# A row-wise log-softmax gradient: loads and stores grouped by two, one row sum moved from VectorE to ScalarE, synchronization by hand

## The chip, the cores and the metric

The kernel runs on one core of one Trainium2 chip. The metric is device time in microseconds (us), lower is better. A profile is one further look at one execution. Its engine names are DVE (VectorE), ACT (ScalarE), POOL (GpSimd) and SP (SyncE, which here only issues transfers; SPq is its queue). The DMA engines are 16 units that share each transfer.

## The reference

`y` and `dy` are float32 of shape 8 x 1024 x 8192, that is 8192 rows of 8192 elements; the output has the same shape.

```python
def reference(y, dy):
    softmax_x = np.exp(y)
    sum_dy = np.sum(dy, axis=-1, keepdims=True)
    return (dy - softmax_x * sum_dy).astype(np.float32)
```

Two inputs are read once and one output is written once: 3 x 268.44 MB = 805.3 MB. No version can move less.

## The kernel before

Rows are taken in G = 32 groups of 256, two rows (R = 2) to a partition. A `dy` tile is 64 KB per partition and has two buffers; the two `y` tiles are 32 KB each. That makes 192 KB of each partition, so a `dy` buffer must be stored before it can be loaded again. All transfers are issued by SyncE on one queue. VectorE takes the negated sums of both rows in one reduction; ScalarE takes the exponential in place; VectorE adds the product to `dy` in place. A framework inserts the waits.

```python
    def load_dy(g):
        dy_t = dyp.tile([P, R * D], fp32, name="dy_t")
        nc.sync.dma_start(out=dy_t[:], in_=dy_v[g])
        s_t = stats.tile([P, R], fp32, name="s_t")
        nc.vector.tensor_reduce(
            out=s_t[:],
            in_=dy_t[:].rearrange("p (r d) -> p r d", r=R),
            axis=mybir.AxisListType.X,
            op=ALU.add,
            negate=True,
        )
        return dy_t, s_t

    def load_y(g):
        y_ts = []
        for r in range(R):
            y_t = yp.tile([P, D], fp32, name="y_t")
            nc.sync.dma_start(out=y_t[:], in_=y_v[g][:, r * D : (r + 1) * D])
            y_ts.append(y_t)
        return y_ts

    def compute(dy_t, s_t, y_ts):
        for r in range(R):
            for c in range(0, D, CD):
                e = y_ts[r][:, c : c + CD]
                d = dy_t[:, r * D + c : r * D + c + CD]
                nc.scalar.activation(e, e, EXP)
                nc.vector.scalar_tensor_tensor(
                    out=d, in0=e, scalar=s_t[:, r : r + 1], in1=d, op0=ALU.mult, op1=ALU.add
                )

    def store(g, dy_t, parts=1):
        w = R * D // parts
        for k in range(parts):
            nc.sync.dma_start(
                out=out_v[g][:, k * w : (k + 1) * w], in_=dy_t[:, k * w : (k + 1) * w]
            )

    cur = load_dy(0)
    for g in range(G):
        if g < G - 1:
            y_ts = load_y(g)
            compute(*cur, y_ts)
            nxt = load_dy(g + 1)
            if g < G - 2:
                store(g, cur[0])
                cur = nxt
            else:
                held, cur = cur, nxt
        else:
            y_ts = load_y(g)
            compute(*cur, y_ts)
            store(g - 1, held[0])
            store(g, cur[0], parts=R)
# (cut: the launch)
```

In the steady state the queue reads: store of group g, the two `y` halves of g+1, `dy` of g+2, then the next store.

## Time and profile before

| | before |
|---|---|
| time, median | 1866.9 us (1866.81 to 1867.58, 3 runs) |
| span of the profiled run | 1865.4 us |
| DMA queue, share of the 16 engines' time | 99.9% |
| mean rate | 432 GB/s |
| VectorE / ScalarE busy | 60% / 25% |

The page of the kernel before: busy time of each engine (us, share of the span, number of instructions), the DMA rows of the 40-slice picture (tenths of busy time, then GB/s), the total, and the queue table (packets, MB, share of the 16 engines).

```profile
DVE 1119.2 (60%) x160; ACT 457.1 (25%) x129; POOL 0.2 (0%) x4
...
DMA  9999999999999999999999999999999999999999
GB/s 427 416 434 431 443 433 422 435 437 436 427 433 431 440 430 434 431 429 441 433 437 425 433 442 431 434 425 436 438 434 433 428 434 437 437 431 430 429 435 396
DMA packets 18582, 805.36 MB, mean 432 GB/s; under 512 B 2064, under 2 KB 2064, under 8 KB 2064
...
q1 hardware_dynamic: 18576, 805.31, 99.9%
...
DMA 74%; DVE 17%; ACT 6%; SPq 1%; issue 1%; DVEq 0%; ACTq 0%
```

The DMA row never leaves 9 and the queue holds the engines 99.9% of the span. VectorE and ScalarE have room. The last line is the chain of waits, followed back from the last instruction, by engine: it gives VectorE 17% of the span.

The timeline of the kernel before over one group (start, duration, engine, line, operation, out<-in, shapes, count; in brackets the idle time just before and what ended it):

```profile
113.31 0.34 SPq L77 DMA_DIRECT2D out_dram<-dy_t  x1
113.75 0.86 SPq L60 DMA_DIRECT2D y_t<-in_y_dram  x2
120.33 17.22 DVE L47 TENSOR_REDUCE s_t<-dy_t 128x2 f32<-128x16384 f32 x1 [7.04 <-DMA dy_t<-in_dy_dram]
139.66 0.33 SPq L45 DMA_DIRECT2D dy_t<-in_dy_dram  x1
```

The store is issued at 113.31 us, while the `dy` load ahead of it is still landing: that landing releases the reduction at 120.33 us. So the store stood in the queue 7.0 us before the previous transfer had landed. The next `dy` load is issued at 139.66 us, when the store has completed; the two `y` loads issued at 113.75 us keep the engines busy until it gets its turn.

### The profile page before, as it was taken

The page shows a single profiled execution, that of the slowest core. Times are in us where ns is not written, and L with a number is a line of the kernel's source. Part 1 is how long each engine was busy: PE and PEld are TensorE (multiplying, and loading weights), DVE is VectorE, ACT ScalarE, POOL GpSimd, SP SyncE. Part 2 cuts the span into 40 slices and gives each one's busy share as a digit, 9 for nine tenths or more (in the row PEclk, how much of TensorE's full clock was granted, in tenths as well). Part 3 has the DMA queues.
Part 4 walks back from the last instruction along what each step waited for, and adds up shares of the span by engine and source line. Part 5 has one row for each costly group of instructions (what it writes and reads, how often), then busy time and mean ns, then how long its engine had stood idle before and what let it go on. Part 6 is the DMA issues. An engine that isn't in the chain of part 4 may idle for free.

```text
span 1865.4 us, 712 instructions
## 1 busy us (share of the span) xinstructions
DVE 1119.2 (60%) x160; ACT 457.1 (25%) x129; POOL 0.2 (0%) x4
## 2 busy tenths in 40 slices
DVE  5675555755557555575555755657656576565664
ACT  2123321233212332123321233212332113331132
POOL 0000000000000000000000000000000000000000
DMA  9999999999999999999999999999999999999999
GB/s 427 416 434 431 443 433 422 435 437 436 427 433 431 440 430 434 431 429 441 433 437 425 433 442 431 434 425 436 438 434 433 428 434 437 437 431 430 429 435 396
DMA packets 18582, 805.36 MB, mean 432 GB/s; under 512 B 2064, under 2 KB 2064, under 8 KB 2064
## 3 DMA queue, kind: packets, MB, share of 16 engines
q1 hardware_dynamic: 18576, 805.31, 99.9%
q14 instruction: 6, 0.05, 0.0%
HBM read 536.87 MB, written 268.44 MB: 432 GB/s over the span
## 4 chain that ended last, share of the span: by engine, by line
DMA 74%; DVE 17%; ACT 6%; SPq 1%; issue 1%; DVEq 0%; ACTq 0%
DMA y_t<-in_y_dram 69%; DVE dy_t L70 15%; ACT y_t L69 6%; DMA dy_t<-in_dy_dram 3%; DVE s_t L47 2%; DMA out_dram<-dy_t 1%; SPq L60 1%; SPq L77 1%; DVEq L122 0%; ACTq L69 0%; DVEq L70 0%
## 5 line engine op out<-in xcount | busy, mean ns | idle before, releaser
L70 DVE SCALAR_TENSOR_TENSOR dy_t<-y_t,s_t,dy_t 128x4096 f32<-128x4096 f32 x128 | 568.1, 4481 | 490.3 <-ACT y_t L69 490.1
L69 ACT ACTIVATE y_t<-y_t 128x4096 f32<-128x4096 f32 x128 | 455.9, 3608 | 1375.6 <-DMA y_t<-in_y_dram 1375.6
L47 DVE TENSOR_REDUCE s_t<-dy_t 128x2 f32<-128x16384 f32 x32 | 551.0, 17220 | 232.1 <-DMA dy_t<-in_dy_dram 232.1
L69 ACT ACT_TABLE_LOAD x1 | 1.3, 1283 | 0.7 <-PEq L111 0.7
L111 POOL MEMSET const-bfloat16-1.0<- 128x1 bf16 x1 | 0.1, 102 | 0.0
L111 POOL MEMSET const-uint8-127<- 128x1 uint8 x1 | 0.1, 102 | 0.0
L111 POOL MEMSET const-float32-1.0<- 128x1 f32 x1 | 0.1, 99 | 0.0
L111 POOL MEMSET const-float32-0.0<- 128x1 f32 x1 | 0.1, 98 | 0.2 <-issue 0.2
## 6 DMA issues: line engine op xcount, KB each, us to landing
y_t<-in_y_dram SPq DMA_DIRECT2D x64, 4096.0 KB, 35.9
out_dram<-dy_t SPq DMA_DIRECT2D x2, 4096.0 KB, 22.6
dy_t<-in_dy_dram SPq DMA_DIRECT2D x32, 38.7
out_dram<-dy_t SPq DMA_DIRECT2D x31, 26.1
```

The lines of the kernel that those rows point to most:

```text
L47: nc.vector.tensor_reduce(out=s_t[:], in_=dy_t[:].rearrange("p (r d) -> p r d", r=R), axis=mybir.AxisListType.X, op=ALU.add, negate=True,)
L60: nc.sync.dma_start(out=y_t[:], in_=y_v[g][:, r * D : (r + 1) * D])
L69: nc.scalar.activation(e, e, EXP)
L70: nc.vector.scalar_tensor_tensor(out=d, in0=e, scalar=s_t[:, r : r + 1], in1=d, op0=ALU.mult, op1=ALU.add)
L77: nc.sync.dma_start(out=out_v[g][:, k * w : (k + 1) * w], in_=dy_t[:, k * w : (k + 1) * w])
L111: nc = _bacc.Bacc("TRN2", target_bir_lowering=False, num_devices=1)
```

## The change

Its intent, as far as the code tells it: (1) load two groups, then store two, so that the traffic changes direction half as often; (2) let ScalarE sum the second row of a partition (a Copy with an accumulated output, into a scratch tile in PSUM, a second on-chip memory beside SBUF, where the other tiles lie), which halves VectorE's reduction; (3) cut the exponential and update into three pieces per row, the first small, so that the two engines overlap sooner; (4) drop the framework's waits for hand-written semaphores. Bytes and SBUF use stay. The core of the diff (removed: `load_dy`, `load_y`, `compute`, `store` and their loop, printed above):

```diff
+    PIECES = [
+        (0, 2048),
+        (2048, 5120),
+        (5120, D),
+        (D, D + 2048),
+        (D + 2048, D + 5120),
+        (D + 5120, W),
+    ]
+    K = len(PIECES)
+    KR = K // R
...  (tiles: x_ts two of [P, W], y_t one of [P, W], copied [P, H] in PSUM; semaphores)
+        for g0 in range(0, G, 2):
+            for j in range(2):
+                g = g0 + j
+                if g >= 2:
+                    nc.sync.wait_ge(out_done[j], 16 * (g // 2))
+                nc.sync.dma_start(out=x_ts[j][:], in_=dy_v[g]).then_inc(dy_in[j], 16)
+                for r in range(R):
+                    if g:
+                        nc.sync.wait_ge(dve_done, K * (g - 1) + KR * (r + 1))
+                    cs = slice(r * D, (r + 1) * D)
+                    nc.sync.dma_start(out=y_t[:, cs], in_=y_v[g][:, cs]).then_inc(y_in[r], 16)
+            for j in range(2):
+                g = g0 + j
+                nc.sync.wait_ge(dve_done, K * (g + 1))
+                nc.sync.dma_start(out=out_v[g], in_=x_ts[j][:]).then_inc(out_done[j], 16)
...
+        for g in range(G):
+            j = g % 2
+            nc.scalar.wait_ge(dy_in[j], 16 * (g // 2 + 1))
+            if g >= 2:
+                nc.scalar.wait_ge(dve_done, K * (g - 2) + 1)
+            for h in range(2):
+                if g or h:
+                    nc.scalar.wait_ge(half_done, 2 * g + h)
+                nc.scalar.activation(
+                    copied[:],
+                    x_ts[j][:, D + h * H : D + (h + 1) * H],
+                    COPY,
+                    accum_out=half_ts[j][:, h : h + 1],
+                ).then_inc(half_done, 1)
+            for k, (b, e) in enumerate(PIECES):
+                if k % KR == 0:
+                    nc.scalar.wait_ge(y_in[k // KR], 16 * (g + 1))
+                nc.scalar.activation(y_t[:, b:e], y_t[:, b:e], EXP).then_inc(exp_done, 1)
+        for g in range(G):
+            j = g % 2
+            x, s, half = x_ts[j], s_ts[j], half_ts[j]
+            nc.vector.wait_ge(dy_in[j], 16 * (g // 2 + 1))
+            nc.vector.tensor_reduce(
+                out=s[:, 0:1], in_=x[:, :D], axis=mybir.AxisListType.X, op=ALU.add, negate=True
+            ).then_inc(sum_done, 1)
+            nc.vector.wait_ge(half_done, 2 * (g + 1))
+            nc.vector.tensor_scalar(
+                out=s[:, 1:2],
+                in0=half[:, 0:1],
+                scalar1=half[:, 1:2],
+                scalar2=-1.0,
+                op0=ALU.add,
+                op1=ALU.mult,
+            ).then_inc(sum_done, 1)
+            nc.vector.wait_ge(sum_done, 2 * (g + 1))
+            for k, (b, e) in enumerate(PIECES):
+                r = b // D
+                nc.vector.wait_ge(exp_done, K * g + k + 1)
+                nc.vector.scalar_tensor_tensor(
+                    out=x[:, b:e],
+                    in0=y_t[:, b:e],
+                    scalar=s[:, r : r + 1],
+                    in1=x[:, b:e],
+                    op0=ALU.mult,
+                    op1=ALU.add,
+                ).then_inc(dve_done, 1)
```

## The prediction

> **What bounds the kernel now.** The 16 DMA engines. The page's queue table gives 805.31 MB on one queue at 99.9% of the 16 engines' time; the mean is 432 GB/s and the DMA row is 9 in all 40 slices. VectorE is busy 60%, ScalarE 25%. The windows view gives 433 GB/s at a DMA share of 1.00 from 1000 to 1116 us. Single DMA records: a 64 KB one takes 2418 ns (median), a 32 KB one 1213 ns. Counts times medians over 16 engines come to 1860 us of the 1865.4 us span. The other 5 us: about 2 at the start, 1 to 2 at the end, and the rest in records above their medians, a quarter of it in the first 116 us. The chain of waits names VectorE for 17%, but other transfers are in flight in those steps. The Trainium skill ("DMA: Bandwidth & Descriptors", section "Where 436 GB/s comes from") puts the ceiling at 435.2 GB/s; by that figure I estimate 1850 us for 805.3 MB, so no reordering could win 1%.
>
> **What the change does.** Bytes, record sizes (but for the last store) and SBUF use stay. The queue alternates loads of two groups with two stores, so directions change half as often. Records above the median at those changes cost about 0.1 us per 58.1 us group, so this saves 1 to 2 us at most. VectorE loses half of each 17.22 us reduction (an estimate of 8.6 us by half the elements); ScalarE gains two 4096-element sums of about 3.6 us each (taking the exponential's 3608 ns); six pieces replace four: from the 4096-element durations I estimate 2.35 and 3.4 us on VectorE for 2048 and 3072 elements, 1.9 and 2.75 us on ScalarE. VectorE falls from 60% to about 47%, ScalarE rises from 25% to about 39%. None of it is on the critical path.
>
> **Does the queue run dry?** At 19.4 us per 8 MB a pair of groups takes 116.2 us. The next pair's first load waits for the first store, while the second still runs: about 17 us to spare; its second dy load has about 38. The second y loads wait for VectorE to finish the same half: about 16 to spare. The tightest is the second store: the last y half lands as the first store starts, and goes through exponential and update in 11 to 13 us, against 19.4: 6 to 8 us to spare. Before, the store had about 7 too (issued at 113.3 us, dy landed at 120.3 us in the timeline). So the DMA stays full.
>
> **Ends.** The last two stores still run back to back. The start gets one more branch and wait on SyncE, under 1 us.
>
> **Predicted:** 1866.0 us, range 1863.0 to 1869.0; faster by over 2%: 0.01, within 2%: 0.98, slower by over 2%: 0.01.
>
> **What would show the steps right or wrong.** Right: queue share 99.9%, mean 432 to 433 GB/s; VectorE near 47%, ScalarE near 39%; two groups in 116 us; SyncE waiting for VectorE and store completions, yet no DMA slice under 9. Wrong: a dip in the DMA row or window shares under 1.00 in mid-run, or other record durations (64 KB not at 2418 ns).
>
> **What would make it wrong.** Pure load or store stretches running at another rate than the mix; sums on ScalarE over 6 us slower per group than thought; a longer start or end.

## More of the kernel before

What SyncE's queue waited for (total us, times, longest us), kernel before:

```profile
SPq L77 <- DVE dy_t L70: 985.9, 32, 35.0
SPq L45 <- DMA out_dram<-dy_t: 742.0, 30, 25.6
```

SyncE waits nearly all the time. That need not cost anything while the engines still have earlier work; how early the next transfer must be issued is measured in experiment 4.

## The result

The kernel after took 1868.1 us in the median (1867.71 to 1868.76, 4 runs) beside 1867.24 us for the kernel before (1866.81 to 1868.3, 4 runs). The ratio is 1.0004, with a 95% interval of 0.9987 to 1.0021: the same. (Ratios here are the mean time of one kernel's fast runs over that of the other's of the same rounds, so not quite the ratio of the medians that are quoted.) A later repetition (in the rounds of experiment 1) gave 1868.0 us beside 1867.75 us.

The same parts of the page, kernel after; also the group lines of the moved work (line, engine, operation, out<-in, shapes, count | busy us, mean ns | idle before, releaser):

```profile
DVE 864.2 (46%) x256; ACT 700.5 (38%) x321; POOL 0.2 (0%) x4
...
DMA  9999999999999999999999999999999999999999
GB/s 426 424 420 438 431 445 429 426 432 444 428 427 436 430 438 434 437 426 433 441 433 431 427 435 438 430 437 427 434 434 443 428 428 432 442 430 431 432 430 397
DMA packets 18438, 805.36 MB, mean 432 GB/s; under 512 B 2048, under 2 KB 2048, under 8 KB 2048
...
q1 hardware_dynamic: 18432, 805.31, 99.9%
...
L115 DVE TENSOR_REDUCE s<-x 128x1 f32<-128x8192 f32 x32 | 277.9, 8686 | 851.0 <-DMA x<-in_dy_dram 851.0
...
L99 ACT ACTIVATE copied<-x 128x4096 f32<-128x4096 f32 x64 | 229.6, 3587 | 977.7 <-DMA x<-in_dy_dram 976.7
...
L99 ACT ACTIVATION_READ_ACCUMULATOR copied<-x 128x1 f32 x64 | 11.9, 186 | 0.0
```

VectorE fell from 1119 to 864 us and ScalarE rose from 457 to 700 us. The DMA lines did not move: 99.9%, 432 GB/s. The single DMA records have the same durations: a 64 KB record takes 2418 ns in the median in both kernels, a 32 KB record 1213 ns before and 1214 ns after.

The timeline of the kernel after around the second store of a pair:

```profile
1012.09 7.22 ACT L108 ACTIVATE y_t<-y_t 128x2048 f32<-128x2048 f32 x3 [2.48 <-DMA y_t<-in_y_dram]
1014.04 2.35 DVE L131 SCALAR_TENSOR_TENSOR x<-y_t,s,x 128x2048 f32<-128x2048 f32 x1 [0.29 <-ACT y_t L108]
1016.69 6.75 DVE L131 SCALAR_TENSOR_TENSOR x<-y_t,s,x 128x3072 f32<-128x3072 f32 x2 [0.30 <-ACT y_t L108]
1023.46 0.34 SPq L85 DMA_DIRECT2D out_dram<-x  x1
1031.41 0.34 SPq L76 DMA_DIRECT2D x<-in_dy_dram  x1
1031.80 1.50 SPq L81 DMA_DIRECT2D y_t<-in_y_dram  x2
1050.71 0.33 SPq L76 DMA_DIRECT2D x<-in_dy_dram  x1
```

The last `y` half lands at 1012.09 us, VectorE finishes at 1023.4 us, and the second store is issued at 1023.46 us. The first store completes at 1031.41 us, which releases the next `dy` load. So the second store is queued 8.0 us ahead of that. Likewise the completion of the second store, at 1050.71 us, releases the second `dy` load of the next pair.

What SyncE's queue waited for, kernel after:

```profile
SPq L81 <- DVE x L131: 793.5, 32, 41.1
SPq L85 <- DVE x L131: 608.0, 16, 38.7
SPq L76 <- DMA out_dram<-x: 376.4, 30, 17.8
```

The waits have other names and lengths than before, and the time is the same.

### The profile page after: what moved, and what is told of

Its sections match the earlier page's. It is cut to its first block, busy times and chain, and to the rows that moved or that the text cites. A ratio compares the mean times of both kernels' runs of the same rounds, so it can differ in the third digit from the quotient of the medians.

```text
span 1865.9 us, 821 instructions
## 1 busy us (share of the span) xinstructions
DVE 864.2 (46%) x256; ACT 700.5 (38%) x321; POOL 0.2 (0%) x4
## 3 DMA queue, kind: packets, MB, share of 16 engines
q1 hardware_dynamic: 18432, 805.31, 99.9%
## 4 chain that ended last, share of the span: by engine, by line
DMA 79%; ACT 8%; DVE 6%; another core or an unknown queue 2%; issue 2%; SPq 1%
DMA y_t<-in_y_dram 42%; DMA out_dram<-x 37%; ACT y_t L108 8%; DVE x L131 6%; SPq L76 0%; SPq L81 0%; SPq L164 0%; SPq L61 0%
## 5 line engine op out<-in xcount | busy, mean ns | idle before, releaser
L115 DVE TENSOR_REDUCE s<-x 128x1 f32<-128x8192 f32 x32 | 277.9, 8686 | 851.0 <-DMA x<-in_dy_dram 851.0
L131 DVE SCALAR_TENSOR_TENSOR x<-y_t,s,x 128x3072 f32<-128x3072 f32 (+1 forms) x192 | 582.3, 3061 | 122.3 <-ACT y_t L108 122.3
L99 ACT ACTIVATE copied<-x 128x4096 f32<-128x4096 f32 x64 | 229.6, 3587 | 977.7 <-DMA x<-in_dy_dram 976.7
L108 ACT ACTIVATE y_t<-y_t 128x3072 f32<-128x3072 f32 (+1 forms) x192 | 461.8, 2468 | 154.2 <-DMA y_t<-in_y_dram 154.2
L99 ACT ACTIVATION_READ_ACCUMULATOR copied<-x 128x1 f32 x64 | 11.9, 186 | 0.0
L119 DVE TENSOR_SCALAR s<-half 128x1 f32<-128x1 f32 x32 | 6.5, 204 | 0.0
```

The lines of the kernel that those rows point to most:

```text
L99: nc.scalar.activation(copied[:], x_ts[j][:, D + h * H : D + (h + 1) * H], COPY, accum_out=half_ts[j][:, h : h + 1],).then_inc(half_done, 1)
L108: nc.scalar.activation(y_t[:, b:e], y_t[:, b:e], EXP).then_inc(exp_done, 1)
L115: nc.vector.tensor_reduce(out=s[:, 0:1], in_=x[:, :D], axis=mybir.AxisListType.X, op=ALU.add, negate=True).then_inc(sum_done, 1)
L119: nc.vector.tensor_scalar(out=s[:, 1:2], in0=half[:, 0:1], scalar1=half[:, 1:2], scalar2=-1.0, op0=ALU.add, op1=ALU.mult,).then_inc(sum_do ...
L131: nc.vector.scalar_tensor_tensor(out=x[:, b:e], in0=y_t[:, b:e], scalar=s[:, r : r + 1], in1=x[:, b:e], op0=ALU.mult, op1=ALU.add,).then_i ...
```

## The experiments

The theory (called theory 1): the DMA engines are full in both kernels, everything that the change moves lies behind them, and each wait of the queue has enough time to spare. The main rival: the change does have effects of some us, and they cancel. A second rival: some of the computation shows in the time, as the chain of waits of the kernel before seemed to say (17% VectorE).

All results were recorded as correct. Times are medians; "before" is the kernel before, run in the same rounds.

### 1. No computation at all

The kernel after with only its transfers, each waiting just for the transfers whose buffer it uses (a wrong result: `out` gets `dy`). All ScalarE and VectorE code is removed, and:

```diff
-                        nc.sync.wait_ge(dve_done, K * (g - 1) + KR * (r + 1))
+                        nc.sync.wait_ge(y_in[r], 16 * g)
...
-                nc.sync.wait_ge(dve_done, K * (g + 1))
+                nc.sync.wait_ge(dy_in[j], 16 * (g // 2 + 1))
```

> The kernel after without any computation: the same transfers in the same order, each waiting only for the transfers whose buffer it uses (wrong result on purpose: out gets dy). Theory (the DMA engines set the time, nothing of the computation is in it): 1864 to 1869 us, within 0.2% of the kernel after. Rival (some of the computation shows, as each wait of the chain suggests): faster by 1% or more.

Measured: 1867.33 us (1866.68 to 1867.66, 6 runs), before 1867.75 us. The unchanged kernel after ran in the same rounds:

> The kernel after once more, unchanged, beside the kernel before and the next three on one chip: 1866 to 1869 us; it sizes the noise for differences of 1 to 2 us.

Measured: 1868.0 us (1867.74 to 1868.53, 6 runs), ratio to before 0.9995 [0.9980, 1.0009].

The page of the version without computation:

```profile
DMA packets 18433, 805.32 MB, mean 432 GB/s; under 512 B 2048, under 2 KB 2048, under 8 KB 2048
...
q1 hardware_dynamic: 18432, 805.31, 99.9%
```

All the computation of the kernel after, 864 us of VectorE and 700 us of ScalarE, is worth 0.7 us of time. The transfers alone are the time: in the kernel after, the sums, the pieces and the waits for them cost no more than that together.

One thing to note: this version was recorded as correct too, although `out` is just `dy`. So the check, as recorded, does not notice a missing computation here, and is no evidence that the computation of the other versions is right.

### 2. The queue order alone

The kernel after with the order of the kernel before:

```diff
-        for g0 in range(0, G, 2):
-            ...  (two groups loaded, two stored)
+        load_dy(0)
+        load_y(0)
+        load_dy(1)
+        for g in range(G - 2):
+            store(g)
+            load_y(g + 1)
+            load_dy(g + 2)
+        load_y(G - 1)
+        store(G - 2)
+        store(G - 1)
```

> The kernel after, with the queue order of the kernel before (loads of one group, then one store). Theory 1 (the DMA engines are full in both orders, all else hides behind them): 1865 to 1870 us, queue share 99.9%, within 0.2% of both kernels. Rival (the paired order gains some us from fewer changes of direction and the new synchronization or the sums lose as much): this one is slower than the kernel after by 3 us or more.

Measured: 1869.68 us (1869.23 to 1869.94, 5 runs), before 1868.11 us, ratio 1.0006 [0.9994, 1.0019]. It is the same as before. The kernel after did not run in these rounds; against its 1868.0 to 1868.1 us elsewhere the difference is 1.6 us, under the 3 us that the rival needed. So there is no hidden pair of opposite effects of that size; one of about 1 us is not excluded. What halving the changes of direction could save at all is read from the DMA records: the time by which records exceed their medians, a mean over the 16 engines, is 4.0 us in the kernel before and 4.0 us in the kernel after, and in mid-run it is 0.00 to 0.02 us (median) per change of direction in both. These medians leave out the few larger cases. Summed from 100 to 1800 us over all records within 2.5 us of a change of direction, the excess is 1.6 us at 58 changes in the kernel before, 0.6 us at 29 changes in the kernel after and 2.3 us at 58 changes in the version tested here. So about 1 us was there to save and was saved at the changes; but the excess elsewhere in these 1700 us rose from 1.2 to 1.7 us and that of the first 100 us from 1.1 to 1.6 us, and the sum stayed at 4.0 us. The version without computation has 4.0 us as well.

### 3. What a record costs

The kernel after with every transfer cut into pieces of 4096 columns (each wait's count is scaled to match):

```diff
-                nc.sync.dma_start(out=x_ts[j][:], in_=dy_v[g]).then_inc(dy_in[j], 16)
+                for c in range(0, W, C):
+                    nc.sync.dma_start(
+                        out=x_ts[j][:, c : c + C], in_=dy_v[g][:, c : c + C]
+                    ).then_inc(dy_in[j], 16)
...  (the same for y and out)
```

> The kernel after with every transfer cut into pieces of 4096 columns, so records of 16 KB instead of 64 and 32 KB. From the medians, 2418 ns for 64 KB and 1213.5 ns for 32 KB, a record costs 9 ns beside its bytes (2 x 1213.5 - 2418): 32768 more data records and 4096 more completion records of 9 ns over 16 engines are +20.7 us, so 1885 to 1892 us, with the queue share still 99.9%. Rival (only bytes count): no change.

Measured: 1883.6 us (1883.54 to 1883.76, 4 runs), ratio 1.0078 [1.0061, 1.0094].

```profile
DMA packets 55304, 805.40 MB, mean 428 GB/s; under 512 B 6144, under 2 KB 6144, under 8 KB 6144
...
q1 hardware_dynamic: 55296, 805.33, 100.3%
```

The time grew by 15.6 us over the kernel after of the same rounds, so records matter beside bytes, but less than expected: 15.6 us x 16 engines / 36864 more records is 6.8 ns each, not 9. (The cut also makes 384 transfers of 128; no run separates the cost of a record from that of a transfer.) The sum of the records' durations did grow by 22 us; they overlap a little here, and the share above 100% shows it. The other direction was tried too: fewer records.

```diff
-                for r in range(R):
+                if j == 0:
                     if g:
-                        nc.sync.wait_ge(dve_done, K * (g - 1) + KR * (r + 1))
+                        nc.sync.wait_ge(dve_done, K * g)
+                    nc.sync.dma_start(out=y_t[:], in_=y_v[g]).then_inc(y_whole, 16)
+                else:
+                    ...  (the two halves, as in the kernel after)
```

> The kernel after with y of the even groups loaded by one transfer of 64 KB records instead of two of 32 KB; the waits for it have more than 3 us to spare. 2048 records of 9 ns over 16 engines fall away: 1.2 us less than the kernel after, 1865 to 1868 us; that is near the noise. If it isn't seen, no version of this order beats both kernels by more than 0.1%.

Measured: 1867.33 us (1866.63 to 1867.86, 6 runs), beside 1868.0 us for the kernel after and 1867.75 us before; the ratio to before is 0.9990 [0.9977, 1.0004]. The sign fits, but the intervals overlap: no version here is shown to beat the kernel before.

### 4. How much spare time there is

If the time is the transfers alone, added VectorE work must cost nothing until a store comes too late. Useless reductions were put ahead of each group's last update:

```diff
+                if k == K - 1:
+                    nc.vector.tensor_reduce(
+                        out=junk[:, 0:1], in_=y_t[:, D : D + 4096], axis=mybir.AxisListType.X, op=ALU.add
+                    )
                 nc.vector.scalar_tensor_tensor(
```

> The kernel after with a useless VectorE reduction of 4096 elements (about 4.4 us) before each group's last update. Theory 1 (the second store has 6 to 7 us to spare): no change, 1866 to 1870 us, though VectorE works 140 us more. Rival (the time of the chain through VectorE counts): +70 us (16 pairs) or +140 us (32 groups).

Measured: 1880.79 us (1877.56 to 1882.28, 4 runs), before 1868.11 us, ratio 1.0062 [1.0046, 1.0077]. This missed: +12.7 us where none was expected. The rival's +70 us or more missed by far more.

> The kernel after with 13.1 us of useless VectorE reductions before each group's last update. Theory 1: only the second store of each pair is late, by 1.3 + 11.4 + 13.1 + 1.3 - 19.4 = 7.7 us, 16 times: about +122 us, so 1980 to 1995 us, and the DMA row dips. Rival (no spare time, each group pays): +420 us; rival (VectorE is hidden wherever it is below 100% busy): no change, since VectorE would be at about 68%.

(Two reductions, of 8192 and 4096 elements.) Measured: 2000.89 us (2000.27 to 2001.44, 4 runs), ratio 1.0709 [1.0695, 1.0724]: +133 us. VectorE is busy 64% and the queue's share falls to 94.5%; the DMA row dips, as expected:

```profile
DMA  9989899898998989999899898999999999898998
...
q1 hardware_dynamic: 18432, 805.31, 94.5%
```

Exposure of one store in each of 16 pairs is right, with 8.3 us each instead of 7.7; both rivals are refuted.

The same spare time can be used up by undoing one part of the change, the sum on ScalarE:

```diff
-            nc.vector.wait_ge(half_done, 2 * (g + 1))
-            nc.vector.tensor_scalar(...)   # and ScalarE's two Copy instructions
+            nc.vector.tensor_reduce(
+                out=s[:, 1:2], in_=x[:, D:], axis=mybir.AxisListType.X, op=ALU.add, negate=True
+            ).then_inc(sum_done, 1)
```

> The kernel after, with both rows' sums on VectorE again (two reductions of 8192 elements, 8.69 us each). Theory 1: the second row's sum delays the updates of the last y half by about 5 us, so the second store of a pair is issued about 16 us after that half lands instead of 11.4 us; with 1.3 us of landing and 1.3 us of starting it is 18.7 us against the 19.4 us of the first store, so the queue just stays full: 1866 to 1871 us. Rival (the sum on ScalarE pays for itself in time now): slower by 10 us or more, over all 16 pairs.

Measured: 1876.83 us (1875.95 to 1878.63, 5 runs), ratio 1.0046 [1.0034, 1.0059]: +8.7 us, between the two expectations. So the ScalarE sum is needed by the paired order: there, the second group's sums fall just ahead of the tight store, the second of the pair. The kernel before has its sums on VectorE without harm, since there a store passes between `dy` and `y`.

Where did the 12.7 us of the 4.4 us delay come from? The page of that version and its timeline at the second store:

```profile
DMA packets 18439, 805.37 MB, mean 428 GB/s; under 512 B 2048, under 2 KB 2048, under 8 KB 2048
...
q1 hardware_dynamic: 18432, 805.31, 99.9%
```

```profile
1018.44 7.22 ACT L109 ACTIVATE y_t<-y_t 128x2048 f32<-128x2048 f32 x3 [3.50 <-DMA y_t<-in_y_dram]
...
1026.37 4.41 DVE L133 TENSOR_REDUCE junk<-y_t 128x1 f32<-128x4096 f32 x1
...
1034.14 0.34 SPq L86 DMA_DIRECT2D out_dram<-x  x1
1037.81 0.34 SPq L77 DMA_DIRECT2D x<-in_dy_dram  x1
```

The store is issued at 1034.14 us, still 3.7 us before the first store completes at 1037.81 us, and the queue's share is still 99.9%. The rate fell to 428 GB/s all the same. The DMA records explain the sum: the excess over the medians is 17.5 us in place of 4.0 us, +13.5 us, about the whole loss. The queue was not empty; records became longer. The 16 engines do not reach the end of a transfer together, so "before it lands" is a wait for the last engine; the first is done some us earlier. From this a second theory was formed: a store must be queued well before the *earliest* engine runs out. It was tested on both kernels:

> The kernel after with 2.3 us of useless VectorE work (a reduction of 2048 elements) before each group's last update. Theory 2, formed from the first four runs (a store must be issued about 1.4 us before the earliest of the 16 engines runs out of records, not before the last): the second store of a pair was issued 5.8 us ahead of the earliest engine's end in the kernel after, 3.5 us are left here, so no change: 1866 to 1870 us. Rival (any delay of the second store costs in proportion, 12 us for 4.4 us): about +6 us.

Measured: 1869.68 us (1869.06 to 1870.83, 5 runs), before 1868.86 us, ratio 1.0000 [0.9987, 1.0013]: no change, as expected. (Three of the eleven runs of the kernel before lay at 1872.9 to 1873.87 us and raise its mean; the medians differ by 0.8 us.)

> The kernel before with the same 2.3 us. Theory 2: its store was issued 2.95 us ahead of the earliest engine's end, 0.7 us are left where 1.4 us are needed, so it begins to cost: 0.2 to 1 us in each of 31 groups, +5 to +35 us. Theory 1 (only the last engine's end counts, 6.25 us before): no change, 1866 to 1870 us.

Measured: 1877.03 us (1875.29 to 1878.86, 6 runs), ratio 1.0039 [1.0025, 1.0053]: +8 us, as the second theory expected and the first did not.

> The kernel before with 4.4 us. Theory 2: the store comes 1.5 us after the earliest engine ran out, in every group: +30 to +90 us, several times the +12 us of the same delay in the kernel after. Theory 1: 18.4 us against 19.4 us, no change.

Measured: 1892.83 us (1889.45 to 1894.69, 4 runs), ratio 1.0121 [1.0104, 1.0138]: +24 us, below the range, but about twice the loss of the kernel after under the same delay.

The edit of the last two is the same reduction in the kernel before:

```diff
                 nc.scalar.activation(e, e, EXP)
+                if r == R - 1 and c + CD == D:
+                    nc.vector.tensor_reduce(
+                        out=junk[:, 0:1], in_=y_ts[r][:, :2048], axis=mybir.AxisListType.X, op=ALU.add
+                    )
```

> The kernel before with 13.1 us. Both theories: every one of 31 stores is late, by about 9 to 10.5 us each with what the switch of direction then costs: +280 to +325 us, so 2145 to 2195 us, against +132 us in the kernel after, where only 16 stores are exposed.

Measured: 1887.61 us (1885.85 to 1889.3, 4 runs), only +19 us. This run does not answer its question. Its timeline shows why (SyncE's issues within one group):

```profile
1064.15 0.34 SPq L86 DMA_DIRECT2D out_dram<-dy_t  x1
1064.58 0.38 SPq L62 DMA_DIRECT2D y_t<-in_y_dram  x1
...
1087.49 0.33 SPq L47 DMA_DIRECT2D dy_t<-in_dy_dram  x1
1090.25 0.33 SPq L62 DMA_DIRECT2D y_t<-in_y_dram  x1
```

One `y` half now goes out after the store, and the other only after the next `dy` load, behind which the following store is queued. The framework's scheduler had ordered this program differently: half of the next group's `y` now comes ahead of each store and fills the time in which the store is late. The experiment would have needed hand-written order, as in experiment 2; it stays undone. The two shorter delays kept the order of the kernel before.

The table puts the runs together. It was worked out from the records of each trace in mid-run: how long before the earliest and the last engine's end of the preceding transfer the tight store, the one with the least time to spare (in the paired order the second of each pair), was issued (median, us; the last engine's end is the landing less 0.5 to 0.8 us), the spread between the 4th and the 13th of the 16 engines at the end of a transfer (median, us), the excess of all records over the medians (us, mean of 16 engines), and the excess around one change from storing to loading (median, us).

```
version              ahead of earliest / last   spread   excess, whole run   at one store->load   time beside before
kernel before             2.95 / 6.25            1.50         4.0                0.00              -
kernel after              5.76 / 7.47            0.79         4.0                0.01              +0.9 us
after, before's order     4.05 / 7.51            1.48         5.3                0.00              +1.6 us
after + 2.3 us            3.05 / 5.28            0.72         4.5                0.03              +0.8 us
before + 2.3 us           1.48 / 4.38            0.44        12.3                0.27              +8.2 us
after, sums on VectorE    1.27 / 4.08            0.56        14.3                0.36              +8.7 us
after + 4.4 us            1.03 / 3.31            0.46        17.5                0.41             +12.7 us
before + 4.4 us           0.89 / 1.99            0.30        25.5                0.76             +24.0 us
after + 13.1 us          -6.20 / -5.33           0.31        29.1                0.84            +132.8 us
```

The loss is the growth of the excess, but for the last two rows, where idle engines come on top (share 99.6% and 94.5%). It starts between 2.95 and 1.48 us ahead of the earliest engine. A late store that finds idle engines sends its first record 0.84 us after its issue, in all 15 mid-run stores of the version with 13.1 us, so simple starvation of the earliest engine would begin near 0.84 us, not at 1.48 (the 1.4 us written in the expectations was an estimate and too high). In the kernel before with 2.3 us the smallest of 29 mid-run leads is still 1.19 us: it lost 8 us although no store came too late for the earliest engine. And the long records do not stand at the late store: they stand where it ends and loads follow, and in the paired order also where loads end and stores follow. Added VectorE work as such, for instance by disturbing the transfers, is not the cause: 1119, 864 and 0 us of it (before, after, no computation) leave the same 4.0 us of excess, and the sums moved back to VectorE cost 8.7 us with about the VectorE work of the kernel before (1127 us beside 1119).

By the spread of the table, taken over all transfers, the versions that lose have their engines closer together (0.30 to 0.56 us) than those that do not (0.72 to 1.50 us). A reading that might fit is that late stores make the early engines wait, so that the engines fall into step, and that a change of direction then meets all 16 at once. That is a guess from a correlation, not shown: no run set the spread by itself, and the correlation hangs on the measure. From the earliest to the last engine at the tight store, two versions that lose have 2.9 and 2.8 us (before + 2.3 us; sums on VectorE), the kernel after, which does not, 1.7 us. Why the records become longer stays open. What is shown is the loss, its size, and that it begins with a store issued less than about 1.5 to 3 us ahead of the earliest engine.

## Why the prediction was right

- **"The 16 DMA engines" bound the kernel.** Shown: without any computation the same transfers take 1867.33 us. The Trainium skill, "DMA: Bandwidth & Descriptors", section "Where 436 GB/s comes from", gives a ceiling of 435.2 GB/s; the 432 GB/s of the span and 433 GB/s of mid-run agree with it, and leave under 1%.
- **"None of it is on the critical path."** Shown by the same run. Shares predicted 47% and 39%, measured 46% and 38%; the reduction predicted 8.6 us, measured 8.69; the sums predicted about 3.6 us, measured 3.59, plus an accumulator read of 0.19 us each that had not been foreseen. The 3.59 us (3587 ns) agrees with the Trainium skill, "ScalarE: Activation LUTs", section "What ACT_TABLE_LOAD costs": 186 ns + 0.833 ns per element, 3598 ns for 4096.
- **"This saves 1 to 2 us at most."** It saved nothing that can be seen in the time. The 0.1 us per group of records above their medians was too high: summed, the changes of direction hold 1.6 us in the kernel before, about 0.05 us per group. Pairing cut that to 0.6 us, but the excess grew elsewhere and its sum stayed at 4.0 us.
- **"6 to 8 us to spare" for the second store.** The figure itself was near: issued 7.5 us before the last engine's end. But it measured the wrong end. Of these, 2.3 us more could be spent freely and 4.4 us could not. Likewise "before, the store had about 7 too ... so the DMA stays full" took both kernels for equally safe. They are not: the kernel before is 2.95 us ahead of the earliest engine, the kernel after 5.76 us. The conclusion, that the DMA stays full, held, and in part by luck: in the kernel after with 4.4 us more the store was still 3.7 us ahead by the prediction's count, and 12.7 us were lost.
- **Predicted 1866.0 us, range 1863.0 to 1869.0; measured 1868.1 us.** Of the 2.1 us, 0.9 are the saving that did not come and 0.3 that the kernel before was at 1867.24 us in these rounds, not 1866.9. The other 0.9 us, between the two kernels, lie within the interval of their ratio.

What the change did buy is room, not time: its tight store comes once in two groups instead of in each, and 2.8 us earlier relative to the earliest engine (1.1 us of these also with the order of the kernel before: 4.05 us in the table). The same 2.3 us of extra VectorE work costs the kernel before 8 us and the kernel after nothing. In the two later sets of rounds, 6 of 22 runs of the kernel before lay between 1871.87 and 1873.87 us, and none of the 6 runs of the unchanged kernel after in one of these sets did, nor of the 6 of its version without computation; whether that is the narrower margin at work was not tested.

## What to carry to other kernels

When the DMA queue is busy 99.9% of the span at its full rate, run the transfers alone before tuning anything else: if they take the whole time, as here, moved computation buys margin at best. What is left to try is fewer bytes or fewer records; no run here showed a gain from the latter. Measure the margin by adding useless work until the time rises, and count it to the first of the 16 engines that runs out, not to the landing. A share of 99.9% does not prove that all is well: compare GB/s and record durations as well, since records can become longer without a gap.

## What the Trainium skill lacked or had wrong

- "HBM Reference", section "Specifications (TRN2)", says that a core streaming alone measures about 425 GB/s. Here one core moved 432 GB/s over the whole span and 433 GB/s in mid-run, with reads and writes on one queue.
- "DMA: Bandwidth & Descriptors", section "Specifications", gives 512 B as the least transfer for line rate; the row does not say what records cost above that. Cutting them from 64 and 32 KB to 16 KB (and 128 transfers to 384) cost 15.6 us in 1868 us, about 6.8 ns per record.
- The same page, section "Latency and other measured facts", gives a first byte after about 600 ns on this path, but not from which moment it counts. Here the first record of a store that found the engines idle began 0.84 us after the start of the issuing instruction, 0.50 us after its end; for the first load of the program it was 1.0 us and 0.6 us. Counted from the end, the figure is near.
- No page gives how far apart the 16 engines end a transfer (1.7 and 2.1 us in two profiles of the kernel after, 3.3 us in the kernel before), or says that stores issued less than about 1.5 to 3 us ahead of the earliest end go with longer records at the changes of direction, by 0.27 to 0.84 us per change from storing to loading.
- "ScalarE: Activation LUTs", section "What it computes", names the accumulator output but not its price: each of the 64 sums was followed by an accumulator read of 186 ns.
